# Two of six down-projection parts by seven block products, with weight sums taken by accumulating transfers

## The chip, the cores and the metric

The kernel runs on one core of a Trainium2 chip. The metric is device time in microseconds of one execution; the time given is the median of several. Names of the profile: PE is TensorE (PEld its weight loads), DVE is VectorE, ACT is ScalarE, POOL is GpSimd and SP is SyncE, whose queue issues most transfers.

## The reference

Two layers of an encoder block on one sequence of 512 tokens with 1024 features, in float32:

```python
def swiglu(x, w_gate, w_up, w_down):
    return (jax.nn.silu(x @ w_gate) * (x @ w_up)) @ w_down

# one layer
x = x + 0.5 * swiglu(rms_norm(x), ...)     # first feed-forward stage
x = x + mixer(rms_norm(x))                 # attention and convolution heads
x = x + 0.5 * swiglu(rms_norm(x), ...)     # second feed-forward stage
x = rms_norm(x)
```

The feed-forward width D_FF is 2816, that is 22 blocks of 128. The change touches the four feed-forward stages (two layers with two each) and leaves the mixer as it is.

## The kernel before

**Precision.** A product in float32 is done as three matmuls of reduced-precision halves (`mm3`, L147 to L153): each operand is split into a high half (a cast) and a low half (the operand less its cast). Weights are split by `split_into` and `load_w`: the cast on ScalarE (L237, L137) into a pool "wh" of 4 buffers of 128x1024, the difference on VectorE (L239, L143) into a pool "wl" of 4. So "high times high", "low times high" and "high times low" stand at L148, L152 and L153.

**Layout.** x, the residual, lies in SBUF as 8 blocks of 128 features by 512 tokens. Matmuls accumulate in PSUM: pool "ps" has 7 banks of 128x512.

**A feed-forward stage** (`ffn_body`, L315) is a row of units u = 0 to 5. Unit 0 makes 2 of the 22 blocks of activations in the ordinary way (`opening`). Units 1 to 5 make 4 blocks each by seven block products in place of eight (`unit`, L442): gate and up weights of the unit form a 2x2 arrangement of blocks a11, a12, a21, a22 (each two tiles of 128x1024 in a pool "fr" of 9), and so do the normalised inputs. Each `product` (L341) is 24 matmuls 128x512, and takes one operand named b11, b21, t1 to t4 or b22 from the input's side (sums of its blocks, made once a stage) and one sum of weight blocks. Before the change `unit` forms these sums with `add` (L334 to L336) on VectorE: a21 += a22, a11 += a21, a12 += a11, and s3 = a11 + a21 into two buffers of a pool "raw" of 3. In units 1 and 2, s3 is instead loaded and the second summand added by an accumulating transfer (L328). Accumulating transfers are issued by GpSimd.

Results of two products are joined (`join`, L360), and gated (`gated`, L370: silu(gate) times up). A block of activations is turned by 32x32 transposes and a round trip through DRAM (`moved`, L381 to L393), and then split in halves (`halved`, L395 to L399).

**The down projection** of a unit's activations runs in the next unit, between that unit's products, through `between(i)`. Activations of units 2 and 3 are taken in units 3 and 4 by `down2` (L523): 4 loads of 512 KB of weights, 8 groups of 12 matmuls 128x512, one group for each feature block of x, and after each group `update` (L509 to L511) adds the bank into x on VectorE, undoing a permutation of tokens as it reads. Activations of units 0 and 1 are taken in unit 2 by `down` with 6 blocks at a time, those of units 4 and 5 at the end of the stage. Those three stay as they are.

**Order.** A scheduler places instructions on each engine when the program is built; what stands in an engine's queue, transfers of SP's and of GpSimd's queue among it, is done in order. `tc.issue_after` holds instructions behind a named one.

The lines that the sums hang on, in `unit` before:

```python
if not first:
    if u > 2:
        add(s3, a11, a21)
    add(a21, a21, a22)
add(a11, a11, a21)
```

Of the kernel before, what the change touches and what calls it, by code (L numbers as in the profile page):

```python
# [38 lines left out]
FRB = 9  # L39
RING = 40  # L40
WIDE = 5
CONV = "DAAD"
PAUSE = 16
LATE = ((), (), (), (0, 1, 2, 3), (4, 5, 6, 7))
SEQ = "q0 R c1 q1 q2 qo k tt kt uq uk c3"
# [21 lines left out]
def encoder_kernel(ctx: ExitStack, tc: tile.TileContext, xT, consts, vecs, rgain, wgu1, wd1,  # L67
                   wcv, wql, wkl, wuq, wkv, wout, wgu2, wd2, wend, gend, out):
    nc = tc.nc
# [240 lines left out]

    def ffn(l, ops, norm, wgu, wd, done, lead=()):
        with tc.tile_pool(name="f", bufs=4) as fpool:
            ffn_body(fpool, l, ops, norm, wgu, wd, done, lead)

    def ffn_body(fpool, l, ops, norm, wgu, wd, done, lead):  # L315
        ending = done is None
# [47 lines left out]

        def gated(t, src, out, N):
            h = N // 2
            for j in range(2):
                r, rh = (v[:, 2 * t + j:2 * t + j + 1] for v in rt)
                A.activation(out[j][:, :h], src[j][:, :h], AF.Silu, scale=r)  # L369
                V.scalar_tensor_tensor(out[j][:, :h], src[j][:, h:N], rh, out[j][:, :h], ALU.mult, ALU.mult)  # L370
            return out
# [8 lines left out]

        def moved(blk):  # L381

            away = dram.tile([2, P, S], FP, tag="d", name=nm("d"))
            for a in range(4):
# [26 lines left out]
        def opening():  # L411
# [14 lines left out]
            rt.extend((norm(), tiny("rh", NT)))  # L426
            V.tensor_scalar(rt[1], rt[0], 0.5, None, ALU.mult)
            vs = []
            for t in range(2):
# [11 lines left out]

        def unit(u, between):  # L442
            first = u == 1
            late = first and bool(lead)
            if first:
                a11 = quarter(u, 0)
                a21 = [fetch(fresh(), FIRST[u] + 4 + h, FIRST[u] + 6 + h) for h in range(2)]
                a12, a22 = quarter(u, 1), quarter(u, 3)
            else:
                with tc.issue_after(order["wd"]) if u == 3 else nullcontext():  # L450
                    a11, a12, a21, a22 = (quarter(u, q) for q in range(4))
            s3 = [wpool.tile([P, WC], FP, tag="raw", name=nm("raw"), bufs=3) for _ in range(2)]
            if first or u == 2:
                for h in range(2):
                    fetch(s3[h], FIRST[u] + h, FIRST[u] + 4 + h)
            N = S
# [5 lines left out]
            product(by, a12, "b21", True, True)  # L462
            if not first:
                if u > 2:
                    add(s3, a11, a21)
                add(a21, a21, a22)
            add(a11, a11, a21)
# [28 lines left out]
            turn(b1, 1, gated(1, d, d, N))  # L496
            if first:
                norm.post()
            between(4)
# [6 lines left out]
            turn(b0, 1, gated(1, bx, [s[:, j * HS:(j + 1) * HS] for j in range(2)], N))  # L506
            return b1 + moved(b0)

        def update(m, pd):  # L509
# [13 lines left out]
        def down2(f0, act, m0):  # L523
            n = len(act)
            w = load_w(wd[l, m0:m0 + 2, :, f0 * P:(f0 + n) * P].rearrange("m p c -> p m c"), 2 * n * P, two=True)
            for i in range(2):
                pd = bank()
                group(pd, [v[:, i * n * P:(i + 1) * n * P] for v in w], act, range(n), n)
                update(m0 + i, pd)

        def weights(i):
# [69 lines left out]
        for u in range(last + 1):  # L601
            f0 = sum(UNITS[:u]) - len(acts)

            def between(i):
                if i == (3 if u == 1 and lead else 0):
                    acts.extend(halved(d) for d in (ds() if u == 1 and lead else ds))
                elif u == 2:
                    down(f0 - UNITS[u - 1], acts, LATE[i])
                elif 1 < u < last:
# [5 lines left out]
            ds = unit(u, between) if u else opening()  # L615
            if 1 < u < last:
# [475 lines left out]
    for l in range(L):  # L1092
        nx, st1, done = follow(l, "gm")
        ffn(l, ops, norm, wgu1, wd1, done, lead if l == 0 else ())
        gx = nx
# [5 lines left out]
        if l + 1 < L:  # L1101
# [9 lines left out]
            ffn(l, ops, norm2, wgu2, wd2, done2)  # L1111
            ops = nops
# [21 lines left out]
        else:  # L1134
            ffn(l, ops, norm2, wgu2, wd2, None)

# [94 lines left out]
```

## Time and profile before

| | us |
|---|---|
| median of 3 runs | 1755.29 (1755.18 to 1757.16) |
| the profiled execution's own time | 1753.08 |
| span of its profile | 1751.0 |
| TensorE busy | 1739.3 |
| VectorE busy | 1392.3 |
| ScalarE busy | 943.8 |
| GpSimd busy | 261.4 |

The span is what lies between the first and the last instruction recorded; 2.08 us of the execution's time lie around it. A group of the profile reads: line, engine, operation, out<-in with partitions and elements, how many, then busy time and mean duration in ns, then idle time of the engine just before them and what ended most of it. A row of the timeline reads: start, duration, engine, line and operation.

### The profile page before, as it was taken

What the parts mean: (1) busy time and instruction counts of PE and PEld (TensorE: products, weight loads), DVE (VectorE), ACT (ScalarE), POOL (GpSimd) and SP (SyncE); (2) the same over time, 40 slices, a digit from 0 to 9 for tenths busy, and PEclk for the clock granted to TensorE, in tenths of its full rate; (3) what the DMA queues carried; (4) which work ended last, traced back from release to release, by engine and by line L of the source; (5) the groups of instructions that cost most, each with busy time, mean ns of one, the idle gap of its engine ahead of it and who ended that gap; (6) DMA issues with size and microseconds to landing.
All of it is one profiled execution on the core that took longest, in us unless ns stands there. A gap on an engine that the chain in (4) does not pass through costs nothing.

```text
span 1751.0 us, 22193 instructions
## 1 busy us (share of the span) xinstructions
PE 1739.3 (99%) x8114; PEld 1446.9 (83%) x8114; DVE 1392.3 (80%) x2039; ACT 943.8 (54%) x1415; POOL 261.4 (15%) x232
## 2 busy tenths in 40 slices
PE   9999999999999999999999999999999999999998
PEld 8888888888788888888888888888888888888887
DVE  8967887589968868778689678766899788678884
ACT  7635545457965544436555344444679555354453
POOL 2000000047931000000100000000579300000000
PEclk9999999999999999999999999999999999999999
DMA  9554435324144554443935345343250545544345
GB/s 321 156 192 145 133 111 149 112 82 129 25 162 127 154 183 145 121 144 94 297 108 172 135 141 158 108 135 113 75 141 17 178 120 158 175 139 133 120 131 158
DMA packets 124509, 245.10 MB, mean 140 GB/s; under 512 B 10992, under 2 KB 59120, under 8 KB 124400
## 3 DMA queue, kind: packets, MB, share of 16 engines
q1 hardware_dynamic: 118928, 226.40, 40.1%
q0 software_dynamic: 4608, 16.78, 5.2%
q8 instruction: 63, 1.03, 0.2%
q10 hardware_dynamic: 864, 0.51, 0.1%
q14 instruction: 46, 0.38, 0.1%
HBM read 216.38 MB, written 25.17 MB: 138 GB/s over the span
## 4 chain that ended last, share of the span: by engine, by line
PE 95%; DVE 2%; DMA 1%; ACT 1%; issue 1%; POOL 0%; SPq 0%; POOLq 0%; DVEq 0%; ACTq 0%
PE ps L148 30%; PE ps L152 29%; PE ps L153 29%; PE ps L895 2%; PE ps L865 2%; PE ps L884 1%; DMA fr<-in_wgu 1%; PE ps L189 0%; DVE wl L239 0%; PE ps L151 0%; PE ps L150 0%; PE ps L850 0%; PE ps L845 0%; PE ps L207 0%; DVE cv L927 0%
## 5 line engine op out<-in xcount | busy, mean ns | idle before, releaser
L152 PE MATMUL ps<-wl,r 128*128 128x512 f32 (+2 forms) x1434 | 546.7, 384 | 0.0
L153 PE MATMUL ps<-wh,r 128*128 128x512 f32 (+2 forms) x1434 | 543.2, 383 | 0.0
L148 PE MATMUL ps<-wh,r 128*128 128x512 f32 (+2 forms) x1434 | 529.4, 384 | 0.4 <-ACT wh L407 0.4
L237 ACT CAST wh<-fr 128x1024 fp32r<-128x1024 f32 x255 | 267.6, 1052 | 273.7 <-PE ps L152 133.4
L239 DVE TENSOR_TENSOR wl<-fr,wh 128x1024 fp32r<-128x1024 f32 x255 | 311.7, 1224 | 78.9 <-ACT wh L237 78.5
L148 PE MATMUL ps<-r,wh 128*128 128x512 f32 x944 | 367.2, 394 | 0.7 <-ACT wh L137 0.7
L152 PE MATMUL ps<-r,wh 128*128 128x512 f32 x912 | 355.3, 390 | 0.0
L153 PE MATMUL ps<-r,wl 128*128 128x512 f32 x912 | 354.7, 389 | 0.0
L148 PEld LDWEIGHTS ps<-wh,r 128*128 128x128 f32 x1434 | 269.4, 188 | 52.3 <-ACT wh L407 0.7
L152 PEld LDWEIGHTS ps<-wl,r 128*128 128x128 f32 x1434 | 269.2, 188 | 52.3 <-DVE wl L239 0.8
L153 PEld LDWEIGHTS ps<-wh,r 128*128 128x128 f32 x1434 | 269.0, 188 | 52.3 <-DVE r L265 0.4
L137 ACT CAST wh<-raw 128x1024 fp32r<-128x1024 f32 (+2 forms) x142 | 139.9, 989 | 187.4 <-issue 69.8
L148 PEld LDWEIGHTS ps<-r,wh 128*128 128x128 f32 x944 | 177.2, 188 | 40.6 <-ACT wh L137 2.0
L152 PEld LDWEIGHTS ps<-r,wh 128*128 128x128 f32 x912 | 171.2, 188 | 37.3 <-issue 1.9
L153 PEld LDWEIGHTS ps<-r,wl 128*128 128x128 f32 x912 | 171.2, 188 | 35.6
L143 DVE TENSOR_TENSOR wl<-raw,wh 128x1024 fp32r<-128x1024 f32 (+2 forms) x130 | 150.4, 1159 | 52.0 <-ACT wh L137 51.6
L935 POOL TENSOR_TENSOR y<-y,pr 128x511 f32<-128x511 f32 (+14 forms) x120 | 157.9, 1316 | 49.3 <-ACT pr L931 41.5
L336 DVE TENSOR_TENSOR fr<-fr,fr 128x1024 f32<-128x1024 f32 x112 | 134.9, 1220 | 15.8 <-DMA fr<-in_wgu 15.8
L511 DVE TENSOR_TENSOR x<-ps,x 128x512 f32<-128x512 f32 x120 | 81.4, 686 | 57.1 <-PE ps L153 56.6
L369 ACT ACTIVATE e<-e,rtok 128x256 f32<-128x256 f32 x120 | 59.8, 507 | 71.6 <-DVE e L360 71.3
L355 ACT COPY e<-ps 128x512 f32<-128x512 f32 x120 | 68.2, 587 | 45.3 <-PE ps L153 44.9
L927 DVE SCALAR_TENSOR_TENSOR cv<-r,vec,cv 128x511 f32<-128x511 f32 (+14 forms) x120 | 88.0, 733 | 5.2 <-ACT cv L923 3.8
(200 smaller groups left out, 1661.5 us busy)
## 6 DMA issues: line engine op xcount, KB each, us to landing
fr<-in_wgu SPq DMA_DIRECT2D x175, 512.0 KB, 4.6
raw<-in_wd SPq DMA_DIRECT2D x56, 512.0 KB, 4.2
d<-e SPq DMA_DIRECT2D x176, 128.0 KB, 2.6
r<-d SPq DMA_DIRECT2D x88, 256.0 KB, 3.1
raw<-in_wd SPq DMA_DIRECT2D x32, 384.0 KB, 4.2
raw<-in_wgu SPq DMA_DIRECT2D x16, 512.0 KB, 8.0
raw<-in_wgu POOLq DMA_DIRECT2D x16, 512.0 KB, 8.7
raw<-in_wcv SPq DMA_DIRECT2D x16, 512.0 KB, 3.2
```

The lines of the kernel that those rows point to most:

```text
L137: A.copy(hi[:, :w], raw[:, :w])
L143: (G if kind in POOLW.split() else V).tensor_tensor(lo[:, :w], raw[:, :w], hi[:, :w].bitcast(FP), ALU.subtract)
L148: T.matmul(o, lh, rh, start=first, stop=False, skip_group_check=free)
L152: T.matmul(o, lh, rl, start=False, stop=False, skip_group_check=free)
L153: return T.matmul(o, ll, rh, start=False, stop=last, skip_group_check=free).ins
L237: order["cast"] = A.copy(hi[:, :w], src[:, :w]).ins
L239: order["lo"] = V.tensor_tensor(lo[:, :w], src[:, :w], hi[:, :w].bitcast(FP), ALU.subtract).ins
L336: V.tensor_tensor(oh, ah, bh, ALU.add)
L355: A.copy(w[:, j, :N], o[j][:, :N])
L511: V.tensor_tensor(xm, pd.rearrange("p (a t j) -> p t a j", a=4, t=NT), xm, ALU.add)
L927: V.scalar_tensor_tensor(acc[:, s:], u[c][:, :S - s], tap(k), acc[:, s:], ALU.mult, ALU.add)
L935: order["conv"] = G.tensor_tensor(acc[:, s:], acc[:, s:], pr[:, s:], ALU.add).ins
```

## The change

For the third and fourth unit of each feed-forward stage (u = 2 and 3, `HALVED`), the down projection of their four blocks of activations is done by seven block products instead of eight groups. Weights and activations form 2x2 blocks: 512 features by 256 activations, and 256 activations by 256 tokens. `sevens` holds the seven products: `run` is one of them, 24 matmuls 128x256 into two banks, and `out` adds the two banks into a quarter of x on VectorE. Products 1, 6, 5 and 3 accumulate one after the other in the same two banks, and `out` reads the running sum after each; products 7 and 4 share another two, product 2 has its own. Signs are put into the activations' split (`apart`), and the first block of a unit carries a minus from its gating (`rt[2]`).

Sums of activations are taken on VectorE (`both`, 4 a unit). Sums of down weights are made in "raw" buffers by `quads`: one load by SP, then accumulating transfers by GpSimd, from new inputs wq1 and wq2 that hold the same weights in another order. One buffer serves products 5, 6 and 3 in turn: it is split, another block is added to it, and so on.

The gate and up weights of units 2 to 5 get their sums in another way and order (`ADDS`, "QVQ"): a11 += a21 by an accumulating transfer, the third product (t3) directly on a11 in place of a buffer of its own and ahead of t2, then a11 += a22 on VectorE, a21 += a22 by transfer, and a12 += a11 by a transfer from SBUF to SBUF. s3 is gone from these units; `unit1` keeps it for u = 1.

`WHEN` tells in which `between(i)` of the next unit each step stands, `BEFORE` what stands ahead of that unit; both count letters for loads and sums, numbers for products.

```diff
+ADDS = (None, None, "QVQ", "QVQ", "QVQ", "QVQ")
+HALVED = (2, 3)
+BEFORE = "SAB"
+WHEN = (("W", "2", "a"), (1,), ("s", "b", 6, "7"), (5,"c",2), (3, "4", 7), (4,))
...
+            def plus(how, ts, q, vs):
+                if how == "V":
+                    return add(ts, ts, vs)
+                for h, t in enumerate(ts):
+                    G.dma_start(out=t, in_=wgu[l, f + 2 * q + h], accum_op=ALU.add)
...
+            product(by, a12, "b21", True, True)
+            plus(how[0], a11, 2, a21)
+            between(1)
...
+            w = splits(a11)
+            plus(how[1], a11, 3, a22)
+            plus(how[2], a21, 3, a22)
+            bz = [bank(), bank()]
+            product(bz, a11, "t3", True, True, w)
+            d = sides(copied(bz, N))
+            between(2)
+            product(bx, a11, "t2", False, True)
+            c = sides(copied(bx, N))
+            for t, v in zip(a12, a11):
+                G.dma_start(out=t, in_=v, accum_op=ALU.add)
...
+            def apart(d, sign, last):
+                hi = slot(FR)
+                lo = d if last else slot(FR)
+                A.activation(hi, d.bitcast(FP), AF.Copy, scale=sign)
+                V.scalar_tensor_tensor(lo, d.bitcast(FP), sign, hi.bitcast(FP), ALU.mult, ALU.subtract)
+                return hi, lo
...
+            def run(o, w, a, start):
+                for m in range(4):
+                    for j in range(2):
+                        c, t = slice((2 * m + j) * P, (2 * m + j + 1) * P), slice(j * HS, (j + 1) * HS)
+                        to = o[m // 2][:, m % 2 * HS:(m % 2 + 1) * HS].rearrange("p (t a j) -> p t a j", t=NT, a=2)
+                        hi, lo = (v[:, t].rearrange("p (a t j) -> p t a j", a=2, t=NT) for v in a)
+                        mm3(to, w[0][:, c], w[1][:, c], hi, lo, start and j == 0 and m % 2 == 0, j == 1, True)
...
+            def out(o, i, k, op):
+                for h in range(2):
+                    xm = x[:, 4 * i + 2 * h:4 * i + 2 * h + 2, :].rearrange("p m (t c) -> p (m t) c", t=NT)
+                    xm = xm[:, :, k * 64:(k + 1) * 64]
+                    V.tensor_tensor(xm, xm, o[h].rearrange("p (q c) -> p q c", c=64), op)
...
+                elif n == "W":
+                    W[5] = split_into("q", W["s"])
+                    quads(((0, 0),), W["s"])
...
+                elif n == "s":
+                    W[6] = split_into("q", W["s"])
+                    quads(((0, 1),), W["s"])
...
+                elif n == 6:
+                    run(O["x"], W[6], apart(B[6], 1.0, False), False)
+                    out(O["x"], 1, 0, ALU.add)
```

In the order of the instructions the change shows at three places. The first is GpSimd's queue in the first feed-forward stage. Before, from the second accumulating transfer of unit 1 on ("raw" is s3, "in_wgu1" the gate and up weights):

```order
L328 DMA raw67_380<-in_wgu1 128x1024
L169 TENSOR_TENSOR rtok55_348<-vtok53_341,minus_half_97 128x4
L328 DMA raw68_381<-in_wgu1 128x1024
L328 DMA raw145_752<-in_wgu1 128x1024
L328 DMA raw146_753<-in_wgu1 128x1024
L678 MEMSET v511_2859 128x8
```

After, in unit 3 ("in_wq1" the down weights, fr234 and fr235 are a21, fr230 and fr231 a11, fr232 and fr233 a12):

```order
L517 DMA fr234_1285<-in_wgu1 128x1024
L607 DMA raw224_1264<-in_wq1 128x1024
L517 DMA fr235_1287<-in_wgu1 128x1024
L517 DMA fr230_1277<-in_wgu1 128x1024
L517 DMA fr231_1279<-in_wgu1 128x1024
L607 DMA raw224_1264<-in_wq1 128x1024
L607 DMA raw273_1498<-in_wq1 128x1024
L545 DMA fr232_1281<-fr230_1277 128x1024
L545 DMA fr233_1283<-fr231_1279 128x1024
L607 DMA raw224_1264<-in_wq1 128x1024
```

Before, the queue goes from unit 2's second sum to the mixer's first fill; after, ten transfers of unit 3 stand in it, and as many of unit 4 behind them.

The second place is VectorE in unit 2 of that stage, from the first split for b21 on. Before (fr137 and fr138 are a11, fr139 and fr140 a12):

```order
L239 TENSOR_TENSOR wl161_811<-fr139_740,wh160_809 128x1024
L336 TENSOR_TENSOR fr137_736<-fr137_736,fr141_744 128x1024
L360 TENSOR_TENSOR e91_508<-ps93_512,e91_508 128x512
L336 TENSOR_TENSOR fr138_738<-fr138_738,fr142_746 128x1024
L379 STREAM_TRANSPOSE e90_477<-t133_720 128x8x32
L239 TENSOR_TENSOR wl163_815<-fr140_742,wh162_813 128x1024
L379 STREAM_TRANSPOSE e90_477<-t133_720 128x8x32
L370 SCALAR_TENSOR_TENSOR e91_508<-e91_508,rh56_350 128x256
L398 TENSOR_TENSOR r113_586<-r113_586,r115_590 128x512
L398 TENSOR_TENSOR r114_588<-r114_588,r116_593 128x512
L239 TENSOR_TENSOR wl166_856<-fr137_736,wh165_854 128x1024
L370 SCALAR_TENSOR_TENSOR e91_508<-e91_508,rh56_350 128x256
```

After (fr138 and fr139 are a11, fr140 and fr141 a12):

```order
L243 TENSOR_TENSOR wl160_807<-fr140_742,wh159_805 128x1024
L383 STREAM_TRANSPOSE e91_479<-t134_722 128x8x32
L364 TENSOR_TENSOR e92_510<-ps94_514,e92_510 128x512
L243 TENSOR_TENSOR wl162_811<-fr141_744,wh161_809 128x1024
L374 SCALAR_TENSOR_TENSOR e92_510<-e92_510,rh56_350 128x256
L408 TENSOR_TENSOR r114_588<-r114_588,r116_592 128x512
L408 TENSOR_TENSOR r115_590<-r115_590,r117_595 128x512
L374 SCALAR_TENSOR_TENSOR e92_510<-e92_510,rh56_350 128x256
L243 TENSOR_TENSOR wl165_850<-fr138_738,wh164_848 128x1024
L383 STREAM_TRANSPOSE e122_634<-e92_510 128x8x32 x2
L243 TENSOR_TENSOR wl167_854<-fr139_740,wh166_852 128x1024
L340 TENSOR_TENSOR fr138_738<-fr138_738,fr144_750 128x1024
```

The two sums into a11 stood between the splits for b21; now there is none, the splits of a11 for t3 (wl165 and wl167) follow, and a sum into a11 stands behind them.

The third place is VectorE in unit 3, where the down projection of unit 2 runs. Before, from the first split of a11 for t2 on:

```order
L239 TENSOR_TENSOR wl263_1426<-fr229_1274,wh262_1424 128x1024
L239 TENSOR_TENSOR wl265_1430<-fr230_1276,wh264_1428 128x1024
L360 TENSOR_TENSOR e245_1326<-e245_1326,ps250_1341 128x512
L360 TENSOR_TENSOR e245_1326<-e245_1326,ps251_1342 128x512
L398 TENSOR_TENSOR r219_1222<-r219_1222,r246_1329 128x512
L398 TENSOR_TENSOR r220_1224<-r220_1224,r247_1332 128x512
L143 TENSOR_TENSOR wl269_1463<-raw267_1459,wh268_1461 128x1024
L370 SCALAR_TENSOR_TENSOR e245_1326<-e245_1326,rh56_350 128x256
L398 TENSOR_TENSOR r227_1270<-r227_1270,r248_1335 128x512
L370 SCALAR_TENSOR_TENSOR e245_1326<-e245_1326,rh56_350 128x256
L398 TENSOR_TENSOR r228_1272<-r228_1272,r249_1338 128x512
L379 STREAM_TRANSPOSE e261_1417<-e245_1326 128x8x32
```

After, from the second row of the join of b11 and b21 on (ps255 and ps256 are the banks of products 1, 6, 5 and 3, r270 is the sum of activations for product 6):

```order
L364 TENSOR_TENSOR e244_1327<-e244_1327,ps250_1340 128x512
L340 TENSOR_TENSOR fr230_1277<-fr230_1277,fr236_1289 128x1024
L243 TENSOR_TENSOR wl264_1425<-fr231_1279,wh263_1423 128x1024
L631 TENSOR_TENSOR r270_1465<-r248_1337,r229_1275 128x512
L631 TENSOR_TENSOR r226_1269<-r226_1269,r229_1275 128x512
L374 SCALAR_TENSOR_TENSOR e244_1327<-e244_1327,rn57_352 128x256
L622 TENSOR_TENSOR x_78<-x_78,ps255_1375 128x8x64
L374 SCALAR_TENSOR_TENSOR e244_1327<-e244_1327,rn57_352 128x256
L622 TENSOR_TENSOR x_78<-x_78,ps256_1376 128x8x64
L340 TENSOR_TENSOR fr231_1279<-fr231_1279,fr237_1291 128x1024
L243 TENSOR_TENSOR wl269_1462<-raw224_1264,wh268_1460 128x1024
L596 SCALAR_TENSOR_TENSOR r272_1469<-r270_1465,r271_1468 128x512
```

Where halves of activations and splits stood, there are now sums of activations (L631), two adds into x (L622), sums into a11 (L340), the split for product 6 (wl269) and, last, the low half of its activations (L596). The first split of a11 for t3 and the first row of the join stand right ahead of these.

More of the change, by code (lines that the diff above doesn't have):

```diff
@@ L379, in turn, with moved @@
                 order["turned"] = V.transpose(to[:, :, (2 * t + j) * 32:(2 * t + j + 1) * 32], v[j][:, :HS]).ins
-        def moved(blk):
+        def moved(blk, keep=False):
             away = dram.tile([2, P, S], FP, tag="d", name=nm("d"))
+            if keep:
+                for a in range(4):
+                    nc.sync.dma_start(
+                        out=away[a // 2].rearrange("(b i) (f c) -> i f b c", i=32, f=2)[:, :, :, a % 2 * P:(a % 2 + 1) * P],
+                        in_=blk[a * 32:(a + 1) * 32].rearrange("i (f b) c -> i f b c", f=2))
+                return away
             for a in range(4):
@@ L440, in opening, with unit1 @@
             return rest if lead else rest()
[L442 to L451, printed above, removed]
+        def unit1(between):
+            u, late = 1, bool(lead)
+            a11 = quarter(u, 0)
+            a21 = [fetch(fresh(), FIRST[u] + 4 + h, FIRST[u] + 6 + h) for h in range(2)]
+            a12, a22 = quarter(u, 1), quarter(u, 3)
             s3 = [wpool.tile([P, WC], FP, tag="raw", name=nm("raw"), bufs=3) for _ in range(2)]
-            if first or u == 2:
-                for h in range(2):
-                    fetch(s3[h], FIRST[u] + h, FIRST[u] + 4 + h)
+            for h in range(2):
+                fetch(s3[h], FIRST[u] + h, FIRST[u] + 4 + h)
             N = S
@@ L462, in unit @@
             product(by, a12, "b21", True, True)
[L463 to L466, printed above, removed]
             add(a11, a11, a21)
@@ L507, in unit @@
             return b1 + moved(b0)
+        def unit(u, between):
+            f = FIRST[u]
+            def plus(how, ts, q, vs):
[3 more added lines that the diff above has]
+                    G.dma_start(out=t, in_=wgu[l, f + 2 * q + h], accum_op=ALU.add)
+            how = ADDS[u]
+            keep = u in HALVED
+            with tc.issue_after(order["wd"]) if u == 3 else nullcontext():
+                a11, a12, a21, a22 = (quarter(u, q) for q in range(4))
+            N = S
+            bx = [bank(), bank()]
+            product(bx, a11, "b11", True, True)
+            a = sides(copied(bx, N))
+            between(0)
+            by = [bank(), bank()]
+            product(by, a12, "b21", True, True)
+            plus(how[0], a11, 2, a21)
+            between(1)
+            join(a, a, by, ALU.add, N)
+            b0 = block()
+            turn(b0, 0, gated(0, a, a, N, keep))
+            w = splits(a11)
[9 more added lines that the diff above has]
+                G.dma_start(out=t, in_=v, accum_op=ALU.add)
+            between(3)
+            product(bx, a21, "t1", False, True)
+            join(d, d, bx, ALU.subtract, N)
+            b1 = block()
+            turn(b1, 1, gated(1, d, d, N))
+            between(4)
+            product(bz, a22, "t4", False, True)
+            join(c, bz, c, ALU.subtract, N)
+            turn(b1, 0, gated(0, c, c, N))
+            b1 = moved(b1, keep)
+            between(5)
+            product(bx, a12, "b22", False, True)
+            s = tmp()
+            turn(b0, 1, gated(1, bx, [s[:, j * HS:(j + 1) * HS] for j in range(2)], N, keep))
+            b0 = moved(b0, keep)
+            return (b1, b0) if keep else b1 + b0
         def update(m, pd):
@@ L602, in ffn_body @@
             f0 = sum(UNITS[:u]) - len(acts)
+            if u - 1 in HALVED:
+                sv = sevens(HALVED.index(u - 1), ds)
+                for n in BEFORE:
+                    sv(n)
             def between(i):
+                if u - 1 in HALVED:
+                    with tc.issue_after(order["cast"]), tc.issue_after(order["lo"]):
+                        for n in WHEN[i]:
+                            sv(n)
+                    return
                 if i == (3 if u == 1 and lead else 0):
@@ L608, in between @@
                     down(f0 - UNITS[u - 1], acts, LATE[i])
-                elif 1 < u < last:
+                elif 1 < u < last and i < 5:
                     m0 = 2 * i - 2
@@ L614, in between @@
                         down2(f0 - UNITS[u - 1], acts, m0)
-            ds = unit(u, between) if u else opening()
+            ds = unit(u, between) if u > 1 else unit1(between) if u else opening()
             if 1 < u < last:
```

96 lines of the change are left out of this document (84 added, 12 removed).

## The prediction

> **What bounds the kernel now.** The page comes first: engine shares, granted clock, transfer queues, then the chain of waits.
>
> ```profile
> span 1751.0 us, 22193 instructions
> PE 1739.3 (99%) x8114; PEld 1446.9 (83%) x8114; DVE 1392.3 (80%) x2039; ACT 943.8 (54%) x1415; POOL 261.4 (15%) x232
> PEclk9999999999999999999999999999999999999999
> q1 hardware_dynamic: 118928, 226.40, 40.1%
> q0 software_dynamic: 4608, 16.78, 5.2%
> PE 95%; DVE 2%; DMA 1%; ACT 1%; issue 1%; POOL 0%; SPq 0%; POOLq 0%; DVEq 0%; ACTq 0%
> ```
>
> The reader is to see that TensorE is busy 99% of the span, at an undiminished clock in all 40 slices, and carries 95% of the chain. VectorE at 80% is the only other engine near a limit. The averages mix stages, so the second view is busy time by stretch, in layer 0's first feed-forward stage: units 3, 4, 5 and 2, and the kernel's first 30 us. (Columns: stretch, length, busy time and instructions of TensorE, its weight loads, VectorE, ScalarE and GpSimd, granted clock, DMA share, GB/s.)
>
> ```profile
> 138.50:198.30 59.80, 59.80 (x265) 49.51 (x264) 47.58 (x61) 27.69 (x37) 0.00 (x0) 1.00 0.45 141
> 198.30:258.20 59.90, 59.90 (x266) 49.61 (x265) 47.42 (x61) 27.88 (x37) 0.00 (x0) 1.00 0.43 132
> 258.20:296.20 38.00, 38.00 (x169) 31.47 (x168) 32.74 (x47) 23.23 (x33) 0.00 (x0) 1.00 0.36 103
> 65.40:138.50 73.10, 73.10 (x322) 59.85 (x321) 57.95 (x78) 33.33 (x46) 0.00 (x0) 1.00 0.47 153
> 0.00:30.00 30.00, 28.51 (x126) 23.80 (x127) 23.68 (x43) 21.99 (x37) 10.05 (x25) 1.00 0.97 338
> ```
>
> In the units that change, TensorE has no idle time to win back. The change can gain only by giving TensorE less work, and lose only by making it wait. Every wait put into these units is new time.
>
> **The change part by part.** First TensorE's work. A unit's four blocks of activations take 8 groups of 12 matmuls 512 wide before, 96 in all, and 7 products of 24 matmuls 256 wide after, 168 in all. What one costs is the distance between starts where TensorE is fed without a gap; the one place with both widths is the kernel's end (timeline: start, duration, engine, line, operation).
>
> ```profile
> 1736.76 0.39 PE L148 MATMUL ps<-wh,r 128*128 128x512 f32 x1
> ...
> 1738.80 0.28 PE L148 MATMUL cv<-wh,r 128*128 128x256 f32 x1
> ...
> 1740.24 0.40 PE L148 MATMUL ps<-wh,r 128*128 128x512 f32 x1
> ```
>
> Nine 512-wide matmuls lie between the first two rows: 2.04 / 9 = 0.2267 us each. Twelve 256-wide ones lie between the last two: 1.44 / 12 = 0.120 us. (The durations, 0.39 and 0.28, overlap and are no price.) A unit's down projection goes from 96 x 0.2267 = 21.76 to 168 x 0.120 = 20.16 us, 1.60 less; with 2 units in each of 4 feed-forward stages that is **-12.8 us**. It breaks even at 21.76 / 168 = 0.1295 us for a 256-wide matmul.
>
> A straight line through the two prices has 0.0133 us that a matmul costs whatever its width, and 0.000417 us a column: splitting the work into narrower matmuls costs little. The quoted 256-wide matmuls stream a contiguous operand; those of the change stream pieces of 32 elements. No row has that form: 0.120 is the lower end, the break-even the place where it matters, and I take 0.120, the nearest row. All 168 load weights for 256 columns of work only, and in the quoted rows that load is covered at 0.120.
>
> The Trainium skill speaks against this step: "TensorE: Matmul & The Clock Gate", section "Back-to-back issue gap", gives a stream of weight load and matmul a sustained 81 ns at 128 columns and 131 ns at 512. By a straight line through these, an estimate, 256 columns take 98 ns and a unit 168 x 0.098 - 96 x 0.131 = 3.9 us more than before, 31 us in all. The trace does not agree: 0.2267 at 512 is 1.7 times that figure, and the ratio of widths here is 1.89 where the page's line has 1.34; the sum goes by the rows. The same section's formula for the isolated gap, N / 2.4 + 2.5 ns, would give 215.8 and 109.2 ns and -2.4 us for a unit, -19 us in all; the trace is 5% and 10% above it.
>
> VectorE and ScalarE next.
>
> ```profile
> L239 DVE TENSOR_TENSOR wl<-fr,wh 128x1024 fp32r<-128x1024 f32 x255 | 311.7, 1224 | 78.9 <-ACT wh L237 78.5
> L336 DVE TENSOR_TENSOR fr<-fr,fr 128x1024 f32<-128x1024 f32 x112 | 134.9, 1220 | 15.8 <-DMA fr<-in_wgu 15.8
> L336 DVE TENSOR_TENSOR raw<-fr,fr 128x1024 f32<-128x1024 f32 x24 | 29.4, 1225 | 17.1 <-DMA fr<-in_wgu 17.0
> L511 DVE TENSOR_TENSOR x<-ps,x 128x512 f32<-128x512 f32 x120 | 81.4, 686 | 57.1 <-PE ps L153 56.6
> L398 DVE TENSOR_TENSOR r<-r,r 128x512 fp32r<-128x512 f32 x88 | 58.2, 687 | 36.5 <-ACT r L397 36.4
> L237 ACT CAST wh<-fr 128x1024 fp32r<-128x1024 f32 x255 | 267.6, 1052 | 273.7 <-PE ps L152 133.4
> ```
>
> By the built programs VectorE loses 88 of the 1220 ns sums (64 of the 112 in the second row, all 24 of the third: 107.6 us) and gains 24 splits of 1224 ns (29.4), 48 more adds into x (112 of 512 elements for 64 updates, 32.9), 24 halves of activations more, and 32 sums of activations (56 at 687 ns by the fifth row, 38.5). Net about -7 us of 1392. But it shifts: a halved unit loses 6 sums of weights and gains 3 splits, 6 adds into x and 7 operations on activations, 13 x 0.687 + 3 x 1.224 - 6 x 1.22 = +5.3 us on 47.58, in a unit of 58.2: 91%. Unit 5 loses its 6 sums and more. ScalarE gains 24 casts and 24 half-size ones, some 40 us on 944, all beside TensorE. Costed at nothing, then, in throughput; in order, below.
>
> Transfers: 120 more accumulating ones, 10 in a halved unit.
>
> ```profile
> fr<-in_wgu SPq DMA_DIRECT2D x175, 512.0 KB, 4.6
> raw<-in_wgu POOLq DMA_DIRECT2D x16, 512.0 KB, 8.7
> fr<-in_wgu POOLq DMA_DIRECT2D x8, 512.0 KB, 9.9
> L328 POOL DMA_DIRECT2D raw<-in_wgu x16 | 14.1, 881 | 99.2 <-DMA raw<-in_wgu 77.3 <-DVE e L370 12.1 <-DVE wl L239 5.5
> DMA to landing us min/median/max: 5.4/8.8/12.4
> ```
>
> The software queue's 5.2% of 1751 us for 32 such transfers is 2.85 us of all 16 engines each. A halved unit then needs 28.5 us beside the 0.45 x 59.8 = 26.9 it has, 55 of 58.2 us. That is below the 0.97 that the kernel's first stretch shows, and so fits, but narrowly: a landing will often be later than 8.8 us (the last row, over the 24 accumulating transfers of one line). GpSimd's issue, 0.88 us, is on an engine that is idle in these units (0.00 above); its queue is in order, though, so a sum whose operand is late holds those behind it. The Trainium skill's "DMA: Bandwidth & Descriptors", section "Anatomy of one DMA — SWDGE (gpsimd) path", fits 2.0 us + bytes / 436,000, an estimate of 3.2 us for 512 KB; the trace's 8.8 is for accumulating transfers beside others, and decides.
>
> **The new waits.** Unit 2 of each stage has the tightest one. The sum a11 + a21 may be taken by transfer only after the first product's split has read a11; the third product then runs directly behind b21.
>
> ```profile
> 601.49 0.62 PE L148 MATMUL ps<-wh,r 128*128 128x512 f32 x2
> ```
>
> ```profile
> 599.65 1.18 DVE L239 TENSOR_TENSOR wl<-fr,wh 128x1024 fp32r<-128x1024 f32 x1
> 600.75 0.68 DVE L360 TENSOR_TENSOR e<-ps,e 128x512 f32<-128x512 f32 x1
> 601.36 1.21 DVE L239 TENSOR_TENSOR wl<-fr,wh 128x1024 fp32r<-128x1024 f32 x1
> 602.48 0.48 DVE L370 SCALAR_TENSOR_TENSOR e<-e,rh 128x256 f32<-128x256 f32 x1
> 602.88 1.22 DVE L336 TENSOR_TENSOR fr<-fr,fr 128x1024 f32<-128x1024 f32 x1
> ```
>
> In layer 0's second feed-forward stage the unit starts (T) at 601.5 with b11's first matmul; b11's two splits, each of one tile of a11, end at T - 0.7 and T + 1.1. A split's end frees the tile for its accumulating transfer. Add 8.8 for landing, 1.05 for the cast, 1.22 for the split: T + 10.4 and T + 12.2. Needed: after 48 matmuls, T + 10.9, and 12 matmuls later, T + 13.6. Before, the sums were VectorE's (the last row is one). So at the median landing nothing waits, at 12.4 us the third product waits 14.0 - 10.9 = 3.1 us. I take 0.5 for each stage, 2 us in all (0 to 12.4); in units 3 and 4 a down-projection product of 24 x 0.120 = 2.9 us stands in front and covers it.
>
> In a halved unit the tight place is the operand of the sixth product, the sum of two activations' blocks. On VectorE its low half stands behind, by the order: 5 operations of 1024 elements, 7 of 512, 2 of 256, which start 1.12, 0.61 and 0.40 us apart in the rows above: 10.7 us. They begin when the first accumulated tile has landed and been cast, at T - 0.7 + 8.8 + 1.05 = T + 9.2, so the half is ready near T + 19.9; TensorE comes to it after b11, b21, the first product and t3, 3 x 5.44 + 2.9 = T + 19.2, with some matmuls of t2 drawn in between. I take 0.4 us a unit, 3 us in all. The lower end is 0; a landing of 9.9, the third row of transfers, makes it 1.5 to 1.8, some 12 to 14 us in all, and 12.4 everywhere would make it 4.3, or 34. The other sums of down weights (split, add, split again in one buffer) have 4 to 5 us to spare at a landing of 8.8.
>
> Sum: -12.8 + 2 + 3 = -7.8 against the profiled execution, 1753.08 us, which gives 1745.3. The median of the runs, 1755.29, stands 2.2 above it, so 1747.5 for the changed kernel. About 0.2%, 3.5 us, is what the measurement tells from no change.
>
> **The rivals.**
> A, the forecast: 1742.5 (no waits at all) to 1751.5 (waits of 9).
> B, the waits eat it: VectorE at 91% and transfers at 95% of a halved unit leave no room for a late landing, and one late operand holds the in-order queue of GpSimd or VectorE. For it speaks the maximum of 12.4 us; against it that most chains have 4 us to spare. With unit 2 at its upper end and the sixth product at the landing of 9.9, some 24 us, the time is 1755.3 - 12.8 + 24 = 1766.5; with every landing at 12.4, 46 us, it would be 1788.5. From 9.3 us of waits on the change is not told from none, from 16.3 us it is slower.
> C, the other side by one mechanism: streaming 32-element pieces, or 168 weight loads, costs TensorE more than 0.1295 us a matmul. At 0.135 it is 22.7 us a unit and +7.4 us, with waits 1767.7; slower by 0.2% from 0.1285 on, with waits of 5 (-1.4 + 5 = +3.6). Against it speaks the quoted 0.120 with the same number of weight columns; for it, that no row streams such pieces.
> D, the larger gain: no waits, and the 256-wide matmuls at the isolated gap's ratio, -19: 1736. Against it, both quoted prices.
>
> **How the numbers follow.** A 0.62, B 0.24 (0.16 not told from none, 0.08 slower), C 0.08 (0.02 not told from none, 0.06 slower), D 0.06. Faster is A and D, 0.68; the other two follow from B and C, 0.18 and 0.14. The time is A's, 1747.5. The range runs from A's lower end to waits of 16.5 us in B, 1742 to 1759, and leaves out D, the far part of B and most of C, 2 in 10; A's own is 1742.5 to 1751.5.
>
> **What would show it.** After, the cadence of matmuls 256 wide in the halved units should be 0.120 us, with 1344 matmuls of that width more. The windows of units 3 and 4 should be 58.2 to 59 us long, VectorE about 52 of them, transfers over 0.8. Idle time of TensorE should stand at t3 of unit 2 (released by the split, it by a transfer from GpSimd's queue) and at the sixth product. The prediction fails if idle time in the halved units exceeds 1 us each, if accumulating transfers land later than 12 us as a rule, or if the cadence is above 0.125.

## The result and the profile after

The changed kernel takes 1831.0 us (median of 4 runs, 1825.93 to 1834.57) against 1755.24 for the kernel before: a ratio of 1.0427, 95% interval 1.0398 to 1.0456. It is 75.8 us slower where 7.8 us faster was forecast. The profiled execution took 1825.93 us with a span of 1824.1. From the page of the changed kernel:

```profile
span 1824.1 us, 23871 instructions
...
PE 1758.9 (96%) x8690; PEld 1479.6 (81%) x8690; DVE 1388.7 (76%) x2083; ACT 979.6 (54%) x1463; POOL 366.0 (20%) x352
...
q0 software_dynamic: 21888, 79.70, 24.4%
...
PE 70%; DMA 13%; DVE 9%; SPq 3%; issue 3%; ACT 2%; POOL 0%; POOLq 0%; DVEq 0%; ACTq 0%
PE ps L152 21%; PE ps L156 21%; PE ps L157 21%; DMA d<-e 9%; DMA r<-d 4%; DVE wl L243 3%; PE ps L1061 2%; PE ps L1031 1%; SPq L395 1%; DVE e L364 1%; ACT wh L241 1%; DVE e L374 1%; PE ps L1050 1%; SPq L390 1%; DVE e L383 1%
...
fr<-in_wgu POOLq DMA_DIRECT2D x72, 512.0 KB, 7.5
d<-e SPq DMA_DIRECT2D x176, 128.0 KB, 4.3
```

TensorE's idle time is 65.2 us (1824.1 - 1758.9) where it was 11.7, and the chain of waits now runs 9% of the span through the transfers d<-e: the writing of activations into DRAM, the first half of the trip that turns them. Before, neither half of it (d<-e, then r<-d for the reading back) is among the fifteen lines of the chain that the page lists. From the page of the kernel before:

```profile
PE ps L148 30%; PE ps L152 29%; PE ps L153 29%; PE ps L895 2%; PE ps L865 2%; PE ps L884 1%; DMA fr<-in_wgu 1%; PE ps L189 0%; DVE wl L239 0%; PE ps L151 0%; PE ps L150 0%; PE ps L850 0%; PE ps L845 0%; PE ps L207 0%; DVE cv L927 0%
...
d<-e SPq DMA_DIRECT2D x176, 128.0 KB, 2.6
r<-d SPq DMA_DIRECT2D x88, 256.0 KB, 3.1
```

The trip is in no term of the forecast.

The longest single wait shows how it works, at the start of unit 2 in layer 0's second feed-forward stage. The chain of waits of the changed kernel between 612 and 645 us (start, length, what):

```profile
618.26 0.53 SPq L395
...
618.83 6.51 DMA d<-e
...
625.92 0.38 SPq L401
...
627.32 0.45 SPq L395
...
627.81 6.22 DMA d<-e
...
634.11 4.29 DMA r<-d
...
638.95 1.05 ACT wh L241
...
640.04 1.22 PE ps L152 x2
```

And of the kernel before at the same place in the program:

```profile
614.95 0.54 SPq L385
615.53 3.49 DMA d<-e
619.10 0.34 SPq L391
619.53 3.63 DMA r<-d
```

A write lands 6.5 us after its issue where it took 3.5, twice in a row, and the activations are there at 638.4. What waits for them is more than the down projection, as ScalarE's timeline in the changed kernel shows:

```profile
628.93 0.62 ACT L407 CAST r<-r 128x512 fp32r<-128x512 f32 x1 [0.22 <-DMA r<-d]
638.42 0.62 ACT L407 CAST r<-r 128x512 fp32r<-128x512 f32 x1 [8.87 <-DMA r<-d]
638.95 1.04 ACT L241 CAST wh<-fr 128x1024 fp32r<-128x1024 f32 x1
```

The cast at L241 belongs to a gate and up product. It stood in ScalarE's queue behind the cast of an activation that had not landed for 8.87 us, and TensorE waited 5.55 us for it. Layer 1 has the same wait in its second stage, 4.75 us; the first stages have none of this length. Then the wait costs a second time (TensorE's timeline, and two windows with the granted clock in the last column but two):

```profile
640.04 1.22 PE L152 MATMUL ps<-wh,r 128*128 128x512 f32 x2 [5.55 <-ACT wh L241]
...
643.17 0.63 PE L157 MATMUL ps<-wh,r 128*128 128x512 f32 x1
643.60 0.63 PE L152 MATMUL ps<-wh,r 128*128 128x512 f32 x1
...
645.52 0.39 PE L157 MATMUL ps<-wh,r 128*128 128x512 f32 x1
645.74 0.39 PE L152 MATMUL ps<-wh,r 128*128 128x512 f32 x1
```

```profile
640.00:645.00 5.00, 4.92 (x11) 3.43 (x12) 4.98 (x8) 4.78 (x8) 0.00 (x0) 0.50 0.00 2
...
660.00:680.00 20.00, 20.00 (x90) 16.54 (x89) 11.44 (x16) 6.48 (x8) 1.76 (x2) 1.00 0.74 198
```

From 640 to 645 us the clock granted is 0.50 and 512-wide matmuls start 0.43 us apart, then 0.22 again. The Trainium skill has this in "TensorE: Matmul & The Clock Gate", section "HAM oscillation — how this bites in real kernels": gaps of more than some 3.4 us bring the slower clock back. The trace agrees on the effect, and shows it after a shorter wait too, in unit 4 of layer 0's first stage, where the spacing of 256-wide matmuls goes from 0.12 to 0.21 us:

```profile
220.49 0.39 PE L156 MATMUL ps<-r,wh 128*128 128x256 f32 x1 [2.64 <-DVE r L596]
220.72 0.28 PE L157 MATMUL ps<-r,wl 128*128 128x256 f32 x1
220.84 0.28 PE L152 MATMUL ps<-r,wh 128*128 128x256 f32 x1
...
222.46 0.41 PE L156 MATMUL ps<-r,wh 128*128 128x256 f32 x1
222.67 0.41 PE L157 MATMUL ps<-r,wl 128*128 128x256 f32 x1
```

Not every such wait has this: after one of 2.27 us, which ends at 776.77, the granted clock from 777 to 780 us is 1.00.

Over the whole span the mean granted clock is 0.987 (0.999 before): 1.2% of 1824 us, some 22 us as an estimate. TensorE's busy time points the same way, 19.6 us more although its matmuls should take 12.8 less. So 73.1 us of span are 53.5 of idle time and 19.6 of busy time. If the 12.8 are saved, 32.4 of busy time are lost, some 22 of them to the lower clock; the rest is not explained here.

Where TensorE waited longest (line, for whom, us in total, times, longest):

```profile
PE ps L156 <- DVE r L596: 21.8, 13, 2.9
PE ps L152 <- ACT wh L241: 12.0, 6, 5.6
...
PE ps L156 <- DVE wl L243: 3.6, 7, 0.6
```

The first line is a second form of the wait, and the larger one in total. L596 makes the low half of an activation operand for the seven products. Eight of its waits, 1.6 to 2.9 us long and 17.2 us in all, are for the first product, one in each halved unit; the other five, 4.6 us, are for the sixth. In VectorE's queue the first product's low half stands behind a sum of activations (L631), which waits for the trip's reads, 38.5 us in all:

```profile
DVE r L631 <- DMA r<-d: 38.5, 8, 5.6
```

### The profile page after: what moved, and what is told of

Read it like the earlier page. It is cut to its first block, busy times and chain, and to the rows that moved or that the text cites. A ratio compares the mean times of both kernels' runs of the same rounds, so it can differ in the third digit from the quotient of the medians.

```text
span 1824.1 us, 23871 instructions
## 1 busy us (share of the span) xinstructions
PE 1758.9 (96%) x8690; PEld 1479.6 (81%) x8690; DVE 1388.7 (76%) x2083; ACT 979.6 (54%) x1463; POOL 366.0 (20%) x352
## 4 chain that ended last, share of the span: by engine, by line
PE 70%; DMA 13%; DVE 9%; SPq 3%; issue 3%; ACT 2%; POOL 0%; POOLq 0%; DVEq 0%; ACTq 0%
PE ps L152 21%; PE ps L156 21%; PE ps L157 21%; DMA d<-e 9%; DMA r<-d 4%; DVE wl L243 3%; PE ps L1061 2%; PE ps L1031 1%; SPq L395 1%; DVE e L364 1%; ACT wh L241 1%; DVE e L374 1%; PE ps L1050 1%; SPq L390 1%; DVE e L383 1%
## 5 line engine op out<-in xcount | busy, mean ns | idle before, releaser
L241 ACT CAST wh<-fr 128x1024 fp32r<-128x1024 f32 x287 | 299.2, 1048 | 247.8 <-PE ps L157 119.4
L156 PE MATMUL ps<-r,wh 128*128 128x512 f32 (+1 forms) x1104 | 387.2, 352 | 22.1 <-DVE r L596 21.8
L152 PE MATMUL ps<-r,wh 128*128 128x512 f32 (+1 forms) x1136 | 396.4, 356 | 10.0 <-ACT r L407 4.3
L243 DVE TENSOR_TENSOR wl<-fr,wh 128x1024 fp32r<-128x1024 f32 x287 | 348.8, 1218 | 73.6 <-ACT wh L241 71.9
L157 PE MATMUL ps<-r,wl 128*128 128x512 f32 (+1 forms) x1104 | 383.1, 351 | 0.0
L156 PEld LDWEIGHTS ps<-r,wh 128*128 128x128 f32 x1104 | 213.1, 193 | 54.6 <-DVE r L596 26.2
L152 PEld LDWEIGHTS ps<-r,wh 128*128 128x128 f32 x1136 | 216.5, 192 | 45.9 <-ACT r L407 6.7
L157 PEld LDWEIGHTS ps<-r,wl 128*128 128x128 f32 x1104 | 212.7, 193 | 25.9
L517 POOL DMA_DIRECT2D fr<-in_wgu x64 | 56.0, 875 | 579.1 <-DMA fr<-in_wgu 263.7
L141 ACT CAST wh<-raw 128x1024 fp32r<-128x1024 f32 (+3 forms) x110 | 105.8, 968 | 116.8 <-PE ps L156 51.7
L147 DVE TENSOR_TENSOR wl<-raw,wh 128x1024 fp32r<-128x1024 f32 (+3 forms) x98 | 111.3, 1137 | 32.7 <-ACT wh L141 32.0
L241 ACT CAST wh<-raw 128x1024 fp32r<-128x1024 f32 x70 | 73.6, 1051 | 71.4 <-PE ps L157 38.0
L408 DVE TENSOR_TENSOR r<-r,r 128x512 fp32r<-128x512 f32 x56 | 38.2, 690 | 88.6 <-ACT r L407 88.2
L243 DVE TENSOR_TENSOR wl<-raw,wh 128x1024 fp32r<-128x1024 f32 x70 | 85.3, 1220 | 20.8 <-ACT wh L241 20.7
```

Source lines behind the costliest of these rows:

```text
L141: A.copy(hi[:, :w], raw[:, :w])
L147: (G if kind in POOLW.split() else V).tensor_tensor(lo[:, :w], raw[:, :w], hi[:, :w].bitcast(FP), ALU.subtract)
L152: T.matmul(o, lh, rh, start=first, stop=False, skip_group_check=free)
L156: T.matmul(o, lh, rl, start=False, stop=False, skip_group_check=free)
L157: return T.matmul(o, ll, rh, start=False, stop=last, skip_group_check=free).ins
L241: order["cast"] = A.copy(hi[:, :w], src[:, :w]).ins
```

## The experiments

Theory 1: accumulating transfers beside the activations' trip hold up its writes, and the queues of SP, ScalarE and TensorE stand behind them. Theory 2: VectorE's longer chain in the halved units makes the waits. Theory 3: the third product waits for its accumulated operand, as the prediction had it.

**One part of the change alone.** e1 takes the sums of gate and up weights as the change does and leaves the down projection in 8 groups; e2 does the opposite.

```diff
 e1
-HALVED = (2, 3)
+HALVED = ()
 e2
-ADDS = (None, None, "QVQ", "QVQ", "QVQ", "QVQ")
+ADDS = (None, None, "VVV", "VVV", "VVV", "VVV")    # and a12 += a11 by add()
```

> The gate and up weights' sums by accumulating transfers (QVQ, t3 in place) alone; the down projection of units 2 and 3 goes back to 8 groups of 12 matmuls. Theory 1 (the activations' trip through DRAM is held up by accumulating transfers: the writes of e into DRAM land in 4 to 10 us where they took 2.6, and ScalarE's and TensorE's queues stand behind them): most of the loss is here, since 6 of the 10 transfers of a unit are, and units 2 and 5 keep theirs: 1785 to 1815 us. Theory 2 (the seven products' chain of sums on VectorE and in the raw buffers makes the waits): near the kernel before, 1750 to 1762. Theory 3 (t3 waits for the accumulated a11, as the prediction had it): 1757 to 1770, with TensorE's waits at t3's split.

> The seven products of the down projection alone; all sums of gate and up weights on VectorE (in the new order, t3 in place). 4 accumulating transfers stay in a halved unit, none in units 2 and 5. Theory 1: the loss of units 2 and 5 goes, some of units 3 and 4 stays; VectorE has about 8 sums in a halved unit again and is close to full there: 1750 to 1780. Theory 2: as slow as the change, 1815 or more. Theory 3: the third product does not wait for a transfer, about 1745 to 1755.

e1: 1823.55 us, ratio 1.0386 (1.0365 to 1.0408), 68 us lost by the gate and up weights' sums, in their new form and order, without any of the seven products: for theory 1, past the upper end that it gave. e2: 1794.64 us, 1.0225 (1.0209 to 1.0241), more than theory 1 allowed it. The parts do not add up (68 + 39 is not 76): e2 puts the sums back on VectorE, which is busy 55.35 of the 61.5 us from 138.5 to 200 us, where a halved unit runs, and TensorE's longest wait in total is then for VectorE (13.8 us for its adds into x). Theory 2 has a share once the transfers are gone.

**The trip's wait taken away.** e3 reads activations from the tiles of the unit before, written long ago; all transfers stay.

```diff
+            old = trips[-3] if len(trips) > 2 else away
...
-                nc.sync.dma_start(out=d.bitcast(FP), in_=away[i])
+                nc.sync.dma_start(out=d.bitcast(FP), in_=old[i])
```

> The changed kernel, but activations are read back from the DRAM tiles of the unit before, which have long been written, so that the reading waits for no write; the writes, all transfers and all arithmetic stay (the activations are of the wrong unit). Theory 1: the waits behind the trip go, and the time falls by 40 us or more, to 1745 to 1785. Theories 2 and 3: nothing in their chains changes, 1820 to 1835.

1773.97 us, 1.0104 (1.0084 to 1.0123): 57 us of the 75.8 go with this one dependency, although the writes still land late (4.8 us in the median). Of TensorE's 21.8 us for the seven products' low halves (L598 in e3), this is left:

```profile
PE ps L156 <- DVE r L598: 1.7, 8, 0.2
```

**The form of the writes.** e4 writes rows of 4 KB in place of pieces of 512 bytes.

```diff
-                    out=away[:, :, a * P:(a + 1) * P].rearrange("f (b i) t -> i (f b) t", i=32),
-                    in_=blk[a * 32:(a + 1) * 32])
+                    out=away.rearrange("f (p r) t -> (f p) (r t)", r=2)[a * 32:(a + 1) * 32],
+                    in_=blk[a * 32:(a + 1) * 32].rearrange("i f c -> i (f c)"))
```

> The changed kernel, but the activations' blocks are written to DRAM in rows of 4 KB, as they lie in SBUF, where it writes pieces of 512 bytes; the bytes, the number of transfers and what waits for what stay (the activations' order is wrong). Theory 1a (a transfer engine takes packets of its queues in turn, so 16 small packets each wait for a large one of the accumulating transfer): the writes' median falls from 4.3 to 3 us or less, and the time by 30 us or more. Theory 1b (the engines are simply busy, and a write gets its share of bytes): writes stay above 4 us, the time within 10 us of 1831.

1810.04 us, 1.0302 (1.0268 to 1.0336): 21 us better, but the median of the writes does not move (4.4 against 4.3). Neither form of the theory had that. The form of a write matters somewhat; it is not the main cause.

**Contention by itself.** e5 and e6 are the kernel before with 6 transfers of 512 KB in each of units 2 to 5, 96 in all, into DRAM tiles that nothing reads: accumulating in e5 (but for the first into each of the 6 tiles), plain in e6.

```diff
+                        p = G.tensor_copy(pin, w[h][1][:, :1].bitcast(FP)).ins
+                        with tc.issue_after(p):
+                            G.dma_start(out=spare[n][:, :WC], in_=wgu[l, FIRST[u] + h], accum_op=ALU.add)   # e6: without accum_op
```

> The kernel before, unchanged in its own work, plus 6 accumulating transfers of 512 KB in each of units 2 to 5 (into DRAM tiles of their own that nothing reads; two each are issued when the splits for b11, b21 and t2 are done; the first use of a tile is a plain write). Nothing waits for them but the queue. Theory 1 (contention with the activations' trip is the main cause): the writes d<-e land in 4 us or more in the median where they took 2.6, and the kernel takes 1780 to 1815. Rival (the changed kernel loses because its own operands come late, by the chain of sums): the writes slow somewhat, the time stays within 10 us, 1750 to 1765.

> As e5, but with plain copies of the same bytes from the same queue instead of accumulating ones. If the accumulation makes a transfer hold the engines long, this costs much less than e5: writes d<-e at 3.3 us or less, 1755 to 1770. If bytes or packets on the engines alone do it: the same as e5 within 10 us.

e5: 1876.24 us, 1.0684 (1.0665 to 1.0704). e6: 1767.01 us, 1.0063 (1.0044 to 1.0081). Of e5, TensorE's longest wait, the software queue's share, and the landing of d<-e:

```profile
PE ps L152 <- ACT r L401: 55.2, 11, 7.2
```

```profile
q0 software_dynamic: 18432, 67.12, 19.7%
```

```profile
DMA to landing us min/median/max: 2.0/7.9/16.8
```

Of e6, the same three:

```profile
PE ps L152 <- ACT r L401: 3.4, 4, 2.4
```

```profile
q0 software_dynamic: 18432, 67.12, 13.7%
```

```profile
DMA to landing us min/median/max: 2.0/4.9/8.7
```

This is the cleanest of the runs: the kernel before, with its own work untouched, loses 120 us to accumulating transfers that nobody waits for, and TensorE waits for the activations' cast. The same bytes without accumulation cost 10 us. Theory 1's direction holds, with double the most that it gave; the price is one for sums into DRAM, where the change's own go into SBUF. e6's time is as expected, its writes are not: 4.9 us in place of 3.3 or less. The queue's time (less 2.85 us for each of the 32 that the kernel before has) is 2.9 us of all engines for an accumulating transfer and 1.6 for a plain one, but that ratio of 1.8 does not explain 120 against 10: in this order a trip with writes at 4.9 us in the median, 8.7 at most, is still covered, and one of 7.9 and 16.8 is not. The median of the writes is no measure of the loss across kernels: the changed kernel has 4.3 (11.5 at most) and loses 76. Whether its longest writes make that difference, or its order of work, which leaves a late activation less time, was not separated. What inside the transfer engines holds a write behind an accumulation stays open.

**Sums on GpSimd.** e7 does the change's six transferred sums of a unit there.

```diff
-ADDS = (None, None, "QVQ", "QVQ", "QVQ", "QVQ")
+ADDS = (None, None, "GVG", "GVG", "GVG", "GVG")    # G: G.tensor_tensor(t, t, v, ALU.add)
```

> The changed kernel with the six weight sums of a unit that it takes by transfer (a11 += a21, a21 += a22, a12 += a11) done by GpSimd as ordinary sums of 128x1024; the four accumulating transfers for the down weights in units 3 and 4 stay. Theory 1: without the transfers in front of the trip most of the loss goes, 1745 to 1765 (GpSimd takes some 3 us for each, 18 of a unit's 58, by the 2971 ns of its one such subtraction in the profile before). Theory 2 (VectorE's chain and the down weights' sums make the waits): 1785 to 1830. If GpSimd and VectorE slow each other at their operands, sums and splits get longer and VectorE becomes the bound: above 1770, with its share over 85%.

1874.28 us, 1.0675 (1.0657 to 1.0693). Writes are back at 2.6 us, and all the same it is slower than the change, against theory 1's range. VectorE's splits get longer beside GpSimd's sums (e7, lines: the splits on VectorE, the sums on GpSimd, TensorE's wait):

```profile
L243 DVE TENSOR_TENSOR wl<-fr,wh 128x1024 fp32r<-128x1024 f32 x287 | 417.3, 1461 | 54.9 <-ACT wh L241 54.1
L518 POOL TENSOR_TENSOR fr<-fr,fr 128x1024 f32<-128x1024 f32 x64 | 173.7, 2724 | 410.3 <-DVE wl L243 348.6 <-DMA d<-e 30.4 <-DMA fr<-in_wgu 30.4
```

```profile
PE ps L156 <- DVE wl L243: 46.4, 34, 4.2
```

A split takes 1461 ns in the mean where it took 1224 (the median is still 1220, the longest 3961), and TensorE waits 46.4 us for splits and 38.2 for the seven products' low halves, also VectorE's. A sum takes GpSimd 2724 ns where VectorE needs 1220; how much of the loss comes from that and how much from the longer splits was not separated. "SBUF — State Buffer" of the Trainium skill, section "SBUF: two separate sides", names a pair of ports that GpSimd and VectorE lock against each other, each for a whole instruction; e7 agrees in so far as the sums it puts on GpSimd lengthen VectorE's operations. The expectation's last clause came true, but with a share of 83% and not over 85%.

**The same transfers at another place.** e8 puts the first sum back on VectorE; e9 is e8 with the transfers of a21 += a22 held until t3's split is done.

```diff
-ADDS = (None, None, "QVQ", "QVQ", "QVQ", "QVQ")
+ADDS = (None, None, "VVQ", "VVQ", "VVQ", "VVQ")
 e9 besides
+            p = G.tensor_copy(pin, w[1][1][:, :1].bitcast(FP)).ins
+            with tc.issue_after(p):
+                plus(how[2], a21, 3, a22)
```

> The changed kernel with the first sum, a11 += a21, on VectorE (two operations a unit more); the other two sums stay transfers, and start after the trip of the unit before has begun. Theory 1: two of the transfers that run beside the trip are gone and t3 waits for none: 1775 to 1805. Theory 3 (t3's late operand alone): all of its share goes, 1750 to 1770. Theory 2: VectorE has more to do in the halved units, no gain, 1825 or more.

> As e8 (first sum on VectorE), and the transfers of a21 += a22 are held back until t3's operand is split, by a one-element copy on GpSimd in front of them; number and kind of transfers are those of e8. Theory 1, in the form that place decides (accumulating transfers cost only where they run beside the activations' trip): 1775 to 1805, 30 us or more under e8. If it is their number: within 10 us of e8's 1838.7.

e8: 1838.73 us, 1.046 (1.0439 to 1.048); e9: 1791.66 us, 1.02 (1.0184 to 1.0216). Two transfers fewer gained nothing in e8, a miss for theory 1 as it was put. VectorE's a11 += a21 has to read a21 before a21's own transfers may start, and so these run into the trip: in unit 2 of layer 0's second stage they are issued at 620.8 and 624.2 us, and the trip's writes begin at 625.1. In the changed kernel they go at 607.4 and 608.7, nine to ten us ahead of the trip (there it is a11's, at 614.1 and 616.2, that run into it), in e9 at 623.7, seven us after its start. Moving the same number of the same transfers gained 47 us. The writes' medians, e8 first:

```profile
d<-e SPq DMA_DIRECT2D x176, 128.0 KB, 4.4
```

```profile
d<-e SPq DMA_DIRECT2D x176, 128.0 KB, 3.2
```

**SP's order, and smaller packets.** e10 puts a unit's writes ahead of all its reads on SP's queue; e11 cuts each accumulating transfer of units 2 to 5 in two of 512 columns.

```diff
 e10
-            return b1 + moved(b0)
+            b0 = moved(b0)
+            return back(b1) + back(b0)      # back() issues the reads
...
 e11
-                G.dma_start(out=t, in_=v, accum_op=ALU.add)
+                for cc in (slice(0, S), slice(S, WC)):
+                    G.dma_start(out=t[:, cc], in_=v[:, cc], accum_op=ALU.add)
```

> The changed kernel, but on SP's queue all writes of a unit's two blocks of activations stand ahead of the first read back. In the changed kernel the reads of the first block stand in front of the second block's writes and hold them until the first block has landed. All transfers and sums stay. If this queue makes a slow write count twice: 1795 to 1815. If the engines alone set the trip: 1825 to 1835, since the second writes then wait there.

> The changed kernel with each accumulating transfer of units 2 to 5 cut into two of 512 columns, so that its packets are half as large, 2 KB; same bytes. If a small packet of a write waits for one packet of an accumulating transfer each time: the writes d<-e get faster, to 3.5 us or less in the median, and the time falls to 1800 or less. If the accumulation itself takes engine time by the byte, or by the packet: the same or slower, 1825 to 1860.

e10: 1838.03 us, 1.0462 (1.0433 to 1.0491); e11: 1834.36 us, 1.0438 (1.0417 to 1.0459). Neither helps, so neither SP's order of writes and reads nor the size of the accumulating packets is what makes the trip late; e10 ends 3 us above the range given for the transfer engines as the limit. In e10 the write's median is 5.1 us.

**What is left with the transfers out of the way.** e12 is e9 in units 3 and 4 only, with units 2 and 5 wholly on VectorE; e13 gives units 2 and 5 the old code; e14 is e12 with e3's early reads.

```diff
 e12
+ADDS = (None, None, "VVV", "VVQ", "VVQ", "VVV")    # and e9's hold
...
 e13
...                                                        # unit_old is unit() of the kernel before
+            ds = (unit_old if u in (2, 5) else unit)(u, between) if u > 1 else unit1(between) if u else opening()
```

> e9's order (first sum on VectorE, a21 += a22 held back behind t3's split) in units 3 and 4 only; units 2 and 5 take all their weight sums on VectorE and have no accumulating transfer of their own. Theory 1: units 2 and 5 return to their lengths before the change, and what remains is the halved units: 1750 to 1770. If it beats the kernel before, the seven products pay once the transfers stand clear of the trip: under 1752. If VectorE (some 55 of 58 us in a halved unit) is the bound then: 1765 to 1780.

> Units 2 and 5 in the code and order of the kernel before (sums on VectorE, t2 ahead of t3, s3 in a buffer of its own); units 3 and 4 as in e12: seven products, first sum on VectorE, a21 += a22 held back behind t3's split. If what e12 has left lies in units 2 and 5 (t3 in place, waiting for VectorE's first sum): 1755 to 1770. If it lies in units 3 and 4: within 8 us of e12's 1784.4.

> e12 with the activations read back from the DRAM tiles of the unit before (activations of the wrong unit), as in e3. If e12's rest is still the trip: 1745 to 1765. If it is VectorE's queue (splits for t3 and the sums of a halved unit): within 10 us of e12's 1784.4.

e12: 1784.36 us, 1.0169 (1.0155 to 1.0183); e13: 1786.02 us, 1.0172 (1.0156 to 1.0189); e14: 1763.63 us, 1.0041 (1.0028 to 1.0054). e12 is above every range given for it, and the old code in units 2 and 5 gains nothing. Some 21 of e12's 28.6 us go when the trip's wait goes, although its writes' median is 3.1 us by then, and 8 remain. TensorE's longest waits in e12, in e13 and in e14:

```profile
PE ps L157 <- DVE wl L244: 17.2, 8, 3.1
```

```profile
PE ps L157 <- DVE wl L244: 25.2, 9, 3.9
```

```profile
PE ps L157 <- DVE wl L244: 10.0, 4, 2.5
```

All three wait longest for VectorE's low half of a gate and up operand, as theory 2 has it: VectorE has the first sum again, and comes late. In e12 part of that is the trip too, since 10.0 of the 17.2 us are left in e14. e13 moves that wait (25.2 us against 17.2) and does not remove it; which part of VectorE's queue causes it was not tried. No version beats the kernel before.

## Why the prediction was wrong

**TensorE's work: right.** In the changed kernel's sixth product 21 matmuls 256 wide start between these two rows, 20 gaps in 2.37 us, 0.1185 each (0.120 forecast, from a contiguous operand):

```profile
168.39 0.28 PE L157 MATMUL ps<-r,wl 128*128 128x256 f32 x1
...
170.76 0.28 PE L157 MATMUL ps<-r,wl 128*128 128x256 f32 x1
```

Pieces of 32 elements cost nothing there, nor do the additional weight loads (576 in the whole kernel); rivals C and D did not come. By this spacing the 12.8 us are there, but no run shows them as time won.

**The accumulating transfers' own landing: right.** 8.8 us was taken, 7.5 measured for the gate and up weights. The wait for them at t3 in unit 2, taken as 0.5 us a stage, did not come: TensorE's seven waits for L243, 3.6 us in all, are all in unit 5. Theory 3 falls.

**The sixth product's operand: near in size.** Forecast were 0.4 us a unit and 3 in all; it came to 4.6 in all, 0 to 1.85 a unit, 0.49 in layer 0's first unit 3 (below). But the working had it from VectorE's order and the accumulated tiles' landing, and with e3's early reads 1.7 us are left, so most of it was the trip: that it came out near is partly luck.

```profile
168.17 0.39 PE L156 MATMUL ps<-r,wh 128*128 128x256 f32 x1 [0.49 <-DVE r L596]
```

The first product, which takes the activations earliest, has no wait in the working; it measured 17.2 us.

**The step that failed** is "Transfers". It summed engine time (55 of 58.2 us), found that it "fits, but narrowly", and asked only when the added transfers land. It did not ask what they do to those already there: the trip's writes went from 2.6 us in the median (5.3 at most) to 4.3 (11.5). The waits' term was 5 us; the time came out 83.6 us above the forecast (75.8 + 7.8), and e3 shows 57 of these to hang on the trip. Of the prediction's signs of failing, one came: idle time above 1 us in every halved unit (2.5 to 4.6 us). The trip's rows stood in the page before, 2.6 us for a write and 3.1 for a read, in units where the working treats activations as simply present. Rival B has the right side (late landings, queues in order) and the wrong transfers: its 1766.5 prices the accumulated operands, not the writes beside them. The second miss is in every wait's price: a wait was put down once, and the lower clock after it cost, by the estimate above, some two fifths as much again (22 us of clock beside 53.5 of idle time).

What stays open is the rest: e3 still loses 18.6 us, and no run took the transfers, VectorE's lateness and the trip away together.

## What to carry to other kernels

When a change adds transfers, list the small transfers that already lie on the way to the busy engine, and ask what each becomes if the new ones run beside it; the added ones' own landing time says nothing of that. An in-order engine that feeds the busy one (here ScalarE) turns one late operand into a wait for products that do not need it. A sum that is free on paper as an accumulating transfer should be tried first as e5 does it, added to the old kernel with nobody waiting.

## What the runs showed of the hardware

Accumulating transfers of 512 KB into DRAM beside other work cost far more than plain ones: 120 us against 10 for 96 transfers in the kernel before, with writes of 128 KB landing in 7.9 us in place of 4.9. GpSimd's sums of 128x1024 lengthen VectorE's splits from 1224 to 1461 ns in the mean. After waits of 5.55 and 2.64 us TensorE's matmuls ran at half speed for some us more, in the first case until 645.
